# The narrow column block of two SwiGLU FFNs moved from last to first, and four seven-product units in every other wide block

## The chip, the cores and the metric

The kernel runs on one core of one Trainium2 chip. The metric is the device time in microseconds; lower is better. Engines are named as in the profile: PE (TensorE matmul), PEld (its weight load), DVE (VectorE), ACT (ScalarE), POOL (GpSimd) and SP (SyncE, which here only issues DMAs).

## The reference, cut to what matters

One layer on 256 tokens of width 2048: a SwiGLU half-step (FFN1), a token mixer, and a second SwiGLU half-step (FFN2). Everything is float32.

```python
D_MODEL, SEQ, D_FF = 2048, 256, 5504
def swiglu(x, w_gate, w_up, w_down):
    return (jax.nn.silu(x @ w_gate) * (x @ w_up)) @ w_down

f1 = swiglu(rms_norm(h, ffn1_pre_norm), ffn1_w_gate, ffn1_w_up, ffn1_w_down)
h = h + 0.5 * rms_norm(f1, ffn1_post_norm)
m = hybrid_token_mixer(rms_norm(h, mix_pre_norm), ...)      # not touched here
h = h + rms_norm(m, mix_post_norm)
f2 = swiglu(rms_norm(h, ffn2_pre_norm), ffn2_w_gate, ffn2_w_up, ffn2_w_down)
h = h + 0.5 * rms_norm(f2, ffn2_post_norm)
```

5504 is 10 x 512 + 384, so ten wide blocks of columns and one narrow one cover the gate and up matrices.

## The kernel before, in words

**Products.** A float32 product is made of three passes (`mm3`, L156 to L160): every operand is split into a rounded part `hi` (ACT, L152 and L279 to L285) and a rest `lo` (DVE, L154 and L244), and PE adds hi x hi, lo x hi and hi x lo. Tokens come in two tiles t of 128. The stationary operand is a 128x128 piece of the transposed input x (`xhi`, `xlo`), and the moving one a row of weights 512 (or 384) columns wide (`whi`, `wlo`). Weights come by DMA into `raw` (issued on SP), five buffers deep (`RING`), as do `whi` and `wlo`; so the splits can run five loads ahead of PE.

**One block of columns.** `gemm_pair` works on gate and up columns f0 to f0+w at once. The inner dimension is 16 pieces of 128, in eight units of two. A plain unit is 8 products, 24 matmuls. A unit with seven products (`Blocks.seven`) treats 2 token tiles x 2 inner pieces x 2 matrices (gate, up) as a two by two block product with seven products instead of eight: 21 matmuls, for which DVE and ACT form sums of weights (`wsum`, `wsumh`, `wsuml`) and the sums of x (`operand_sums`, kept as `hkhi`, `hklo`) must be there. `SUMS` are three such units (2, 4, 6) and `FOUR` are four (2, 4, 5, 6). `share` and `close` add the shared products into the accumulators `c` at a block's end.

**The order of blocks.** `ffn` goes through f0 = 0, 512, ..., 5120; the narrow block is the last. The first block of each FFN has plain units alone, since the sums of x are formed while it runs: 192 matmuls. In FFN1 (`begin` is given) it is a `gemm_pair` whose first loads are issued at the program's start by `begin`, while x is loaded, transposed and normalised piece by piece (`first_norm`). In FFN2 the gate half goes first through all inner pieces for t=0 and then for t=1 (`gemm_block` with `held`), while the norm of t=1 still runs, and the up half follows. After that, FFN1 has `SUMS` in blocks 1, 3, 5, 7, 9 and `FOUR` in 2, 4, 6, 8 and 10 (the narrow one); FFN2 has `FOUR` in 1, 3, 5, 7, 9 and `SUMS` in 2, 4, 6, 8 and 10 (narrow). A `SUMS` block is 183 matmuls, a `FOUR` block 180.

**After a block.** `finish` multiplies silu(gate) by up on DVE (L704), splits the result into 16 bit halves (ACT, L708), transposes them by a DMA that ACT issues (`turned`, L712), and copies them into `hT` (ACT, L717). `side` spreads such steps over the loads of the next block. Behind the last block there is no next block: `side.flush()` in `down_proj` takes the remaining steps after its second load. `down_proj` then multiplies `hT` by the down weights, inner piece by inner piece; pieces 6 and 7 are its first unit with seven products.

**What sets the order.** The program is written as above, and a scheduler gives each engine its queue, in order, when the kernel is built. A queue's instructions run in order, so one that waits holds up those behind it.

Of the kernel before, what the change touches and what calls it, by code (L numbers as in the profile page):

```python
# [7 lines left out]
F32 = mybir.dt.float32  # L8
# [8 lines left out]
P = 128  # L17
D = 2048
NT = 2
KT = D // P  # L20
DFF = 5504
FKT = DFF // P
EPS = 1e-6
CB = 512
GATE_NORMALIZER = 16.0
# [7 lines left out]
SUMS = (2, 4, 6)  # L33
FOUR = (2, 4, 5, 6)
# [53 lines left out]
def kernel(ctx: ExitStack, tc: tile.TileContext, a: dict, out: bass.AP):  # L88
# [15 lines left out]
    def nm(s):  # L104
        uid[0] += 1
        return f"{s}_{uid[0]}"
# [217 lines left out]
    def first_of(w_dram, c0, w=CB):  # L324
        def chunk(i):
            return wchunk(w_dram[2 * i * P:2 * (i + 1) * P, c0:c0 + w]
                          .rearrange("(k p) c -> p k c", p=P), w)
        return chunk
# [59 lines left out]
    def rstd(ss, n, width, tag):  # L388

        v = small.tile([P, width], F32, tag=f"{tag}v", name=nm("v"))  # L390
        nc.gpsimd.tensor_scalar(v, ss, 1.0 / n, EPS, op0=ALU.mult, op1=ALU.add)
        r = small.tile([P, width], F32, tag=f"{tag}r", name=nm("r"))
# [283 lines left out]
    def ffn(pre, x, rs, post, pre_next, begin=None, ready=(), then=None):  # L676
        with ExitStack() as fctx:
            fwork = fctx.enter_context(tc.tile_pool(name=nm("fwork"), bufs=2, reuse_waits="tile"))
            fpool = fctx.enter_context(tc.tile_pool(name=nm("fpool"), bufs=1, reuse_waits="tile"))
# [10 lines left out]
            raws = begin(x_sums) if begin else ()  # L690
# [4 lines left out]
                return [(hi, lo)]  # L695

            xl = lhs_of(x)
            hT = []

            fours = 0 if begin else 1  # L700

            def finish(t, f0, w, u, s):
                n = w // P
# [12 lines left out]
                src = turned[:, :2 * n, :].rearrange("p (h j) k -> p h j k", h=2)  # L716
                nc.scalar.activation(dst.rearrange("p j (k h) -> p h j k", h=2), src, AF.Copy)  # L717

            for f0 in range(0, DFF, CB):
                w = min(CB, DFF - f0)  # L720
                f1 = f0 + w
                w1 = min(CB, DFF - f1)
                following = [first_of(a[pre + s], f1, w1) for s in ("_w_gate", "_w_up") if w1]
                if f0 or begin:
                    g, u, ready = gemm_pair(
                        [(a[pre + "_w_gate"], f0), (a[pre + "_w_up"], f0)], w, xl, sums, ready,
                        following, () if f0 else raws,
                        (FOUR if f0 // CB % 2 == fours else SUMS) if f0 else ())
                else:
                    g = gemm_block(a[pre + "_w_gate"], f0, w, xl, held=held, ready=ready)  # L730
                    ready = ()
                s = []
                for t in range(NT):
                    st = fwork.tile([P, CB], F32, tag="silu", name=nm("silu"))
                    nc.scalar.activation(st[:, :w], g[t][:, :w], AF.Silu, scale=rs[t])
                    s.append(st)
                if not (f0 or begin):
                    side.spawn(x_sums())
                    u = gemm_block(a[pre + "_w_up"], f0, w, xl)
                hT.append(fpool.tile([P, 4, NT * P], F32, tag="hT", name=nm("hT"), bufs=11))  # L740
                for t in range(NT):
                    side.spawn(finish(t, f0, w, u[t], s[t]))
            def lhs():
                parts = {}

                def get(t, kt):
                    g2 = kt // 2
                    if g2 not in parts:
                        n = min(2, FKT - g2 * 2)
                        hi, lo = new_part(0), new_part(1)  # L750
# [34 lines left out]
            def ys():  # L785
                return fwork.tile([P, CB], F32, tag=ytags.pop(), name=nm("y"))

            return down_proj(a[pre + "_w_down"], FKT, lhs, sums_of, post, pre_next,
                             [wpost[:, n, :] for n in range(4)], ys,
# [488 lines left out]
    x, rs = new_xT(), [None, None]  # L1278

    def begin(x_sums):  # L1280

        raws = []

        def load_h(*tns):
            for t, n in tns:
                nc.sync.dma_start(h[t][n], a["x"][t * P:(t + 1) * P, n * CB:(n + 1) * CB])

        def load_w(*ics):
            for i, c in ics:
                raws.append(wload(a[("ffn1_w_gate", "ffn1_w_up")[i]]  # L1290
                                  [2 * c * P:2 * (c + 1) * P, :CB]
                                  .rearrange("(k p) c -> p k c", p=P), CB, apart=not (i or c)))

        load_h((0, 0))
        load_w((0, 0))
        load_h((1, 0))
        load_w((1, 0), (0, 1))
        load_h((0, 1))
        load_w((1, 1))
        load_h((1, 1))  # L1300
        load_w((0, 2))
        load_h((0, 2), (1, 2), (0, 3), (1, 3))

        idle = work.tile([P, CB], F32R, tag="tmp", name="idle", bufs=3)
        nc.gpsimd.memset(idle.bitcast(F32), 0.0)
        ps = ps_tile()

        def idling(n):
            for _ in range(n):
                nc.tensor.matmul(ps, lhsT=idle[:, :P], rhs=idle, start=True, stop=True)  # L1310

        idling(9)
        tp = ps_tile()
        nc.tensor.transpose(tp[:, :KT], wrow, ident[:KT, :KT])
        first_ops.append(nc.vector.tensor_copy(wcol, tp[:, :KT]))
        side.spawn(first_norm(x, rs, idling, x_sums))
        return raws

    x, rs, ready = ffn("ffn1", x, rs, "ffn1_post_norm", wcols[:, 1, :], begin,
                       then=first_of(a["w_in"], O_GQ))  # L1320
    x, rs, ready = mixer(x, rs, ready, first_of(a["ffn2_w_gate"], 0))
    ffn("ffn2", x, rs, "ffn2_post_norm", None, ready=ready)
    side.flush()

# [45 lines left out]
```

## Time and profile before

| | us |
|---|---|
| median of 3 runs | 2069.73 (2069.12 to 2075.82) |
| the profiled execution: time | 2072.41 |
| the profiled execution: span from the first to the last instruction | 2070.3 |
| PE busy | 2054.9 |
| DVE busy | 1849.8 |
| ACT busy | 1303.3 |

The times are device microseconds of whole executions; the span is that of the one profiled execution. A stretch "A:B" is in microseconds from the span's start. In a row of the timeline stand the start, the duration, the engine, the line, the operation, what it writes and reads, how many are merged, and in brackets how long the engine idled before it and what ended that. A matmul's duration is longer than the distance to the next one, since they overlap in the array; the distance of two starts is what one costs.

### The profile page before, as it was taken

The page shows a single profiled execution, that of the slowest core. Times are in us where ns is not written, and L with a number is a line of the kernel's source. Part 1 is how long each engine was busy: PE and PEld are TensorE (multiplying, and loading weights), DVE is VectorE, ACT ScalarE, POOL GpSimd, SP SyncE. Part 2 cuts the span into 40 slices and gives each one's busy share as a digit, 9 for nine tenths or more (in the row PEclk, how much of TensorE's full clock was granted, in tenths as well). Part 3 has the DMA queues.
Part 4 walks back from the last instruction along what each step waited for, and adds up shares of the span by engine and source line. Part 5 has one row for each costly group of instructions (what it writes and reads, how often), then busy time and mean ns, then how long its engine had stood idle before and what let it go on. Part 6 is the DMA issues. An engine that isn't in the chain of part 4 may idle for free. (4 is left out here: it accounts for less than half of the span.)

```text
span 2070.3 us, 28990 instructions
## 1 busy us (share of the span) xinstructions
PE 2054.9 (99%) x10337; PEld 1701.7 (82%) x10337; DVE 1849.8 (89%) x2187; ACT 1303.3 (63%) x1714; POOL 40.7 (2%) x87
## 2 busy tenths in 40 slices
PE   9999999999999999999999999999999999999998
PEld 7888888888888888878888888888888888888886
DVE  7899998998999879989999897577998999989996
ACT  6666666666666576576655554465666666666663
POOL 1000000000000100000000000010000000000000
PEclk9999999999999999999999999999999999999999
DMA  8776767767667467556565566756767767686663
GB/s 268 204 221 209 242 187 222 217 189 236 212 197 229 153 193 231 163 169 191 171 200 192 180 220 216 220 187 183 219 212 210 214 213 244 176 239 196 217 209 130
DMA packets 246105, 423.50 MB, mean 205 GB/s; under 512 B 63476, under 2 KB 71863, under 8 KB 245960
## 3 DMA queue, kind: packets, MB, share of 16 engines
q1 hardware_dynamic: 194896, 401.80, 61.6%
q10 hardware_dynamic: 51064, 19.84, 4.8%
q8 instruction: 81, 1.33, 0.3%
q14 instruction: 64, 0.52, 0.1%
HBM read 406.11 MB, written 4.19 MB: 198 GB/s over the span
## 5 line engine op out<-in xcount | busy, mean ns | idle before, releaser
L154 DVE TENSOR_TENSOR wlo<-raw,whi 128x1024 fp32r<-128x1024 f32 (+3 forms) x498 | 586.0, 1191 | 83.6 <-ACT whi L152 82.5
L152 ACT ACTIVATE whi<-raw 128x1024 fp32r<-128x1024 f32 (+3 forms) x498 | 507.1, 1031 | 228.9 <-PE c L159 66.2
L158 PE MATMUL c<-whi,xhi 128*128 128x512 f32 (+1 forms) x1270 | 494.0, 389 | 0.0
L160 PE MATMUL c<-wlo,xhi 128*128 128x512 f32 (+1 forms) x1270 | 490.7, 387 | 0.4 <-DVE wlo L154 0.4
L159 PE MATMUL c<-whi,xlo 128*128 128x512 f32 (+1 forms) x1270 | 490.4, 386 | 0.0
L244 DVE TENSOR_TENSOR wlo<-raw,whi 128x1024 fp32r<-128x1024 f32 (+1 forms) x252 | 295.9, 1204 | 35.9 <-ACT whi L283 23.1
L160 PEld LDWEIGHTS c<-wlo,xhi 128*128 128x128 f32 x1270 | 238.4, 188 | 48.0 <-DVE wlo L154 0.9
L158 PEld LDWEIGHTS c<-whi,xhi 128*128 128x128 f32 x1270 | 238.4, 188 | 46.6 <-ACT xhi L470 0.6
L159 PEld LDWEIGHTS c<-whi,xlo 128*128 128x128 f32 x1270 | 238.5, 188 | 45.6
L283 ACT ACTIVATE whi<-raw 128x1024 fp32r<-128x1024 f32 (+1 forms) x126 | 131.6, 1044 | 199.1 <-DVE raw L244 99.6
L244 DVE TENSOR_TENSOR wsuml<-wsum,wsumh 128x1536 fp32r<-128x1536 f32 (+1 forms) x126 | 217.9, 1729 | 8.1 <-ACT wsumh L285 8.1
L160 PE MATMUL c<-wlo,hkhi 128*128 128x512 f32 x558 | 217.2, 389 | 2.4 <-DVE wlo L154 2.0
L159 PE MATMUL c<-whi,hklo 128*128 128x512 f32 x558 | 216.9, 389 | 0.2 <-DVE hklo L154 0.2
L158 PE MATMUL c<-whi,hkhi 128*128 128x512 f32 x558 | 216.8, 389 | 0.0
L281 ACT ACTIVATE wsumh<-wsum 128x1024 fp32r<-128x1024 f32 (+1 forms) x126 | 131.1, 1040 | 88.3 <-DVE wsum L244 65.9
L279 ACT ACTIVATE whi<-raw 128x1024 fp32r<-128x1024 f32 (+1 forms) x126 | 130.9, 1039 | 60.0 <-PE c L159 44.9
L244 DVE TENSOR_TENSOR wsum<-raw,raw 128x1024 f32<-128x1024 f32 (+1 forms) x126 | 151.7, 1204 | 17.8 <-DMA raw<-in_ffn_w_down_dram 13.1
L160 PEld LDWEIGHTS c<-wlo,hkhi 128*128 128x128 f32 x558 | 104.7, 188 | 25.4 <-DVE wlo L154 2.4
L159 PEld LDWEIGHTS c<-whi,hklo 128*128 128x128 f32 x558 | 104.7, 188 | 22.2 <-DVE hklo L154 0.6
L158 PEld LDWEIGHTS c<-whi,hkhi 128*128 128x128 f32 x558 | 104.7, 188 | 21.4
L244 DVE TENSOR_TENSOR c<-c,psum 128x512 f32<-128x512 f32 (+1 forms) x135 | 86.4, 683 | 10.6 <-PE c L160 10.4
L244 DVE TENSOR_TENSOR wsum<-raw 128x512 f32<-128x512 f32 (+1 forms) x126 | 86.1, 683 | 3.6
(346 smaller groups left out, 3156.8 us busy)
## 6 DMA issues: line engine op xcount, KB each, us to landing
raw<-in_ffn_w_down_dram SPq DMA_DIRECT2D x124, 512.0 KB, 5.1
raw<-in_w_in_dram SPq DMA_DIRECT2D x104, 512.0 KB, 4.5
raw<-in_ffn_w_up_dram SPq DMA_DIRECT2D x97, 512.0 KB, 4.4
raw<-in_ffn_w_gate_dram SPq DMA_DIRECT2D x96, 512.0 KB, 4.7
raw<-in_ffn_w_gate_dram SPq DMA_DIRECT2D x128, 256.0 KB, 4.0
raw<-in_w_in_dram SPq DMA_DIRECT2D x128, 256.0 KB, 3.5
raw<-in_ffn_w_up_dram SPq DMA_DIRECT2D x126, 256.0 KB, 3.8
raw<-in_ffn_w_down_dram SPq DMA_DIRECT2D x96, 256.0 KB, 3.6
```

Source lines behind the costliest of these rows:

```text
L152: last[0] = nc.scalar.activation(hi, src, AF.Copy)
L154: nc.vector.tensor_tensor(lo, src, hi.bitcast(F32), op=ALU.subtract)
L158: nc.tensor.matmul(ps, lhsT=xhi, rhs=whi, start=start, stop=False)
L159: nc.tensor.matmul(ps, lhsT=xlo, rhs=whi, start=False, stop=False)
L160: nc.tensor.matmul(ps, lhsT=xhi, rhs=wlo, start=False, stop=stop)
L244: return nc.vector.tensor_tensor(o, x, y, op=op)
L279: nc.scalar.activation(ahi, ra, AF.Copy)
L281: nc.scalar.activation(hi[:, 0:2, :], wsum[:, 0:2, :], AF.Copy)
L283: nc.scalar.activation(bhi, rb, AF.Copy)
```

## The change

Both FFNs take the 384 wide block (columns 5120 to 5503) first and then the ten wide ones. Blocks are counted by j, their place in the order: block 0 is narrow and plain; blocks 1, 3, 5, 7, 9 have `FOUR`, blocks 2, 4, 6, 8, 10 `SUMS`, in both FFNs. The loads at the program's start and those that the mixer issues ahead for FFN2 are those of the narrow block.

```diff
+FIRST = DFF // 512 * 512
...
-            hT = []
-            fours = 0 if begin else 1
+            hT = {}
+            blocks = [FIRST] + list(range(0, FIRST, CB))
...
-            for f0 in range(0, DFF, CB):
+            for j, f0 in enumerate(blocks):
                 w = min(CB, DFF - f0)
-                f1 = f0 + w
-                w1 = min(CB, DFF - f1)
-                following = [first_of(a[pre + s], f1, w1) for s in ("_w_gate", "_w_up") if w1]
-                if f0 or begin:
+                following = [first_of(a[pre + s], f1) for f1 in blocks[j + 1:j + 2]
+                             for s in ("_w_gate", "_w_up")]
+                if j or begin:
                     g, u, ready = gemm_pair(
                         [(a[pre + "_w_gate"], f0), (a[pre + "_w_up"], f0)], w, xl, sums, ready,
-                        following, () if f0 else raws,
-                        (FOUR if f0 // CB % 2 == fours else SUMS) if f0 else ())
+                        following, () if j else raws, (FOUR if j % 2 else SUMS) if j else ())
...
-                hT.append(fpool.tile([P, 4, NT * P], F32, tag="hT", name=nm("hT"), bufs=11))
+                hT[f0 // CB] = fpool.tile([P, 4, NT * P], F32, tag="hT", name=nm("hT"), bufs=11)
...
-                                  [2 * c * P:2 * (c + 1) * P, :CB]
+                                  [2 * c * P:2 * (c + 1) * P, FIRST:]
...
-    x, rs, ready = mixer(x, rs, ready, first_of(a["ffn2_w_gate"], 0))
+    x, rs, ready = mixer(x, rs, ready, first_of(a["ffn2_w_gate"], FIRST, DFF - FIRST))
```

Line numbers of the changed kernel are mostly one higher (L154 becomes L155, L244 becomes L245). Of units with seven products FFN1 had 31 wide and 4 narrow ones, FFN2 32 wide and 3 narrow; each now has 35 wide ones. Every engine issues as many instructions as before; 21 matmuls that were 512 columns wide are now 384 wide.

Three places in the queues matter below. In the rows, `c`, `p` are accumulators in PSUM, `raw` loaded weights, and the numbers are the builder's.

DVE around the start of FFN1's second block, before: the sums of x (`sums`, `hklo`) are through ahead of the first block's product with silu (L704).

```order
L154 TENSOR_TENSOR hklo_569<-sums_501,hkhi_568 128x512
L207 TENSOR_TENSOR sums_630<-sums_572,sums_630 128x128
L154 TENSOR_TENSOR wlo_577<-raw_574,whi_576 128x1024
L154 TENSOR_TENSOR wlo_583<-raw_580,whi_582 128x1024
L154 TENSOR_TENSOR hklo_654<-sums_630,hkhi_653 128x512
L154 TENSOR_TENSOR wlo_638<-raw_635,whi_637 128x1024
L244 TENSOR_TENSOR wsum_681<-raw_679,raw_680 128x1024
L244 TENSOR_TENSOR raw_680<-wsum_681,raw_679 128x512
L154 TENSOR_TENSOR wlo_664<-raw_661,whi_663 128x1024
L704 SCALAR_TENSOR_TENSOR silu_586<-c_17_154,r_414,silu_586 128x512
```

And now, the same place on DVE:

```order
L155 TENSOR_TENSOR hklo_569<-sums_501,hkhi_568 128x512
L206 SCALAR_TENSOR_TENSOR sums_630<-sums_630,sums_572 128x128
L245 TENSOR_TENSOR wsum_663<-raw_661,raw_662 128x1024
L155 TENSOR_TENSOR wlo_583<-raw_580,whi_582 128x1024
L705 SCALAR_TENSOR_TENSOR silu_586<-c_17_154,r_414,silu_586 128x384
L705 SCALAR_TENSOR_TENSOR silu_588<-c_19_156,r_421,silu_588 128x384
L208 TENSOR_TENSOR sums_630<-sums_572,sums_630 128x128
L155 TENSOR_TENSOR wlo_638<-raw_635,whi_637 128x1024
L245 TENSOR_TENSOR raw_662<-wsum_663,raw_661 128x512
L245 TENSOR_TENSOR wsum_663<-raw_662 128x512
L245 TENSOR_TENSOR wlo_671<-raw_661,whi_670 128x1024
L155 TENSOR_TENSOR hklo_654<-sums_630,hkhi_653 128x512
```

The third load of the second block (`wlo_638`) and the last sums of x now stand behind the product with silu, which waits for the first block's last matmul.

DVE at the end of FFN1's gate and up work, before: one load of the down weights (`wlo_4115`) is split ahead of the closing of the block, the next three behind it.

```order
L154 TENSOR_TENSOR wlo_4115<-raw_4112,whi_4114 128x1024
L244 TENSOR_TENSOR psum_4064<-psum_4064,p_812_3842 128x384
L244 TENSOR_TENSOR c_789_3762<-c_789_3762,psum_4064 128x384
L244 TENSOR_TENSOR psum_4065<-psum_4064,p_811_3841 128x2x384
L244 TENSOR_TENSOR c_791_3764<-c_791_3764,psum_4064 128x384
L244 TENSOR_TENSOR c_790_3763<-c_790_3763,psum_4065 128x384
L244 TENSOR_TENSOR c_792_3765<-c_792_3765,psum_4065 128x384
L704 SCALAR_TENSOR_TENSOR silu_4098<-c_790_3763,r_414,silu_4098 128x384
L704 SCALAR_TENSOR_TENSOR silu_4100<-c_792_3765,r_421,silu_4100 128x384
L154 TENSOR_TENSOR wlo_4137<-raw_4134,whi_4136 128x1024
L154 TENSOR_TENSOR wlo_4165<-raw_4162,whi_4164 128x1024
L154 TENSOR_TENSOR wlo_4187<-raw_4184,whi_4186 128x1024
```

And now (`wlo_4115` is the row just before these):

```order
L155 TENSOR_TENSOR wlo_4137<-raw_4134,whi_4136 128x1024
L245 TENSOR_TENSOR psum_4064<-psum_4064,p_816_3866 128x512
L155 TENSOR_TENSOR wlo_4165<-raw_4162,whi_4164 128x1024
L245 TENSOR_TENSOR psum_4064<-psum_4064,p_818_3868 128x512
L155 TENSOR_TENSOR hklo_4278<-hT_1306,hkhi_4277 128x512
L245 TENSOR_TENSOR psum_4065<-psum_4064,p_817_3867 128x1024
L245 TENSOR_TENSOR c_792_3770<-c_792_3770,psum_4064 128x512
L245 TENSOR_TENSOR c_794_3772<-c_794_3772,psum_4064 128x512
L245 TENSOR_TENSOR c_793_3771<-c_793_3771,psum_4065 128x512
L155 TENSOR_TENSOR wlo_4187<-raw_4184,whi_4186 128x1024
L245 TENSOR_TENSOR c_795_3773<-c_795_3773,psum_4065 128x512
L705 SCALAR_TENSOR_TENSOR silu_4098<-c_793_3771,r_414,silu_4098 128x512
```

Four loads of the down weights are split ahead of the product with silu, where one was.

ACT at the same place, before (`whi_4259` and `wsumh_4253` belong to the first seven-product unit of the down weights):

```order
L708 ACTIVATE halves_4156<-silu_4100 128x768
L712 DMA_TRANSPOSE turned_4154<-halves_4152 128x6x128
L712 DMA_TRANSPOSE turned_4158<-halves_4156 128x6x128
L152 ACTIVATE whi_4234<-raw_4232 128x1024
L717 ACTIVATE hT_4102<-turned_4154 128x2x3x128
L717 ACTIVATE hT_4102<-turned_4158 128x2x3x128
L279 ACTIVATE whi_4259<-raw_4250 128x1024
```

And now:

```order
L709 ACTIVATE halves_4156<-silu_4100 128x1024
L713 DMA_TRANSPOSE turned_4154<-halves_4152 128x8x128
L713 DMA_TRANSPOSE turned_4158<-halves_4156 128x8x128
L153 ACTIVATE held_4207<-sums_4202 128x512
L153 ACTIVATE whi_4234<-raw_4232 128x1024
L718 ACTIVATE hT_4102<-turned_4154 128x2x4x128
L718 ACTIVATE hT_4102<-turned_4158 128x2x4x128
L280 ACTIVATE whi_4259<-raw_4250 128x1024
```

The order is the same but for `held_4207`; the transposes and the copies into `hT` are a third larger.

More of the change, by code (lines that the diff above doesn't have):

```diff
@@ L736, in ffn @@
                     s.append(st)
-                if not (f0 or begin):
+                if not (j or begin):
                     side.spawn(x_sums())
                     u = gemm_block(a[pre + "_w_up"], f0, w, xl)
-                hT.append(fpool.tile([P, 4, NT * P], F32, tag="hT", name=nm("hT"), bufs=11))
+                hT[f0 // CB] = fpool.tile([P, 4, NT * P], F32, tag="hT", name=nm("hT"), bufs=11)
                 for t in range(NT):
@@ L1290, in load_w @@
                 raws.append(wload(a[("ffn1_w_gate", "ffn1_w_up")[i]]
-                                  [2 * c * P:2 * (c + 1) * P, :CB]
-                                  .rearrange("(k p) c -> p k c", p=P), CB, apart=not (i or c)))
+                                  [2 * c * P:2 * (c + 1) * P, FIRST:]
+                                  .rearrange("(k p) c -> p k c", p=P), DFF - FIRST,
+                                  apart=not (i or c)))
         load_h((0, 0))
```

## The prediction

> **What bounds the kernel.** I read the page first, then the distance of matmul starts in the timeline, then the stretches of the single blocks, and last the waits at the blocks that move.
>
> ```profile
> span 2070.3 us, 28990 instructions
> PE 2054.9 (99%) x10337; PEld 1701.7 (82%) x10337; DVE 1849.8 (89%) x2187; ACT 1303.3 (63%) x1714; POOL 40.7 (2%) x87
> PEclk9999999999999999999999999999999999999999
> ```
>
> PE is busy nearly throughout at a clock that is always granted, so time is saved by fewer or shorter matmuls, or by taking out places where PE waits. DVE, at 89%, is the next engine. What one matmul costs is the distance of starts in an undisturbed piece. The first and the last of 72 wide ones, and of 24 narrow ones:
>
> ```profile
> 1712.25 0.39 PE L158 MATMUL c<-whi,xhi 128*128 128x512 f32 x1
> 1728.34 0.39 PE L160 MATMUL c<-wlo,xhi 128*128 128x512 f32 x1
> 454.31 0.33 PE L158 MATMUL c<-whi,xhi 128*128 128x384 f32 x1
> 458.29 0.33 PE L160 MATMUL c<-wlo,xhi 128*128 128x384 f32 x1
> ```
>
> A wide one costs 16.09/71 = 0.2266 us, a narrow one 3.98/23 = 0.1730; 128 columns are worth 0.054. With these prices every block can be checked. The stretches run from a block's first matmul to the next one's; FFN1's rows come first (block 0, 1, 9, the narrow block, the first six pieces of the down product, its first seven-product unit), then FFN2's (block 0, 1, 2, 3, narrow, the six pieces, the unit).
>
> ```profile
> core 0: us, PE busy (x) PEld busy (x) DVE busy (x) ACT busy (x) POOL busy (x), PEclk, DMA share, GB/s
> 7.11:54.32 47.21, 47.21 (x221) 38.71 (x221) 41.73 (x59) 34.73 (x56) 6.22 (x10) 1.00 0.83 277
> 54.32:96.25 41.93, 41.93 (x187) 34.47 (x185) 34.56 (x36) 26.08 (x29) 0.00 (x0) 1.00 0.78 217
> 383.89:425.37 41.48, 41.48 (x185) 34.35 (x183) 39.73 (x43) 27.25 (x32) 0.00 (x0) 1.00 0.74 216
> 425.37:458.47 33.10, 32.31 (x182) 31.09 (x180) 30.82 (x41) 23.86 (x32) 0.00 (x0) 1.00 0.65 183
> 458.47:477.13 18.66, 16.65 (x73) 13.44 (x73) 13.43 (x21) 12.49 (x16) 0.00 (x0) 1.00 0.67 204
> 477.13:482.36 5.23, 5.15 (x22) 3.79 (x21) 5.23 (x5) 3.04 (x4) 0.00 (x0) 1.00 0.77 246
> 1383.09:1429.06 45.97, 45.97 (x213) 37.92 (x212) 40.23 (x53) 29.47 (x45) 5.66 (x12) 1.00 0.57 172
> 1429.06:1470.65 41.59, 41.39 (x181) 33.63 (x180) 33.75 (x33) 25.32 (x27) 0.00 (x0) 1.00 0.68 198
> 1470.65:1512.13 41.48, 41.48 (x184) 34.36 (x183) 39.47 (x41) 28.19 (x32) 0.00 (x0) 1.00 0.76 233
> 1512.13:1552.93 40.80, 40.80 (x181) 33.79 (x180) 38.67 (x40) 27.33 (x31) 0.00 (x0) 1.00 0.66 200
> 1800.17:1832.92 32.75, 32.34 (x184) 31.59 (x183) 30.20 (x39) 23.81 (x33) 0.00 (x0) 1.00 0.75 214
> 1832.92:1849.49 16.57, 16.53 (x74) 13.34 (x73) 11.78 (x20) 8.84 (x12) 0.00 (x0) 1.00 0.96 222
> 1849.49:1856.03 6.54, 5.76 (x22) 3.81 (x22) 5.87 (x6) 6.54 (x9) 0.00 (x0) 1.00 0.76 258
> ```
>
> A wide `SUMS` block is 183 x 0.2266 = 41.47 us and takes 41.48; a wide `FOUR` block is 180 x 0.2266 = 40.79 and takes 40.80. Both lose nothing, though DVE is at 95% to 96% in them. The narrow block of FFN1 is 180 x 0.1730 = 31.14 and takes 33.10: 1.96 lost. That of FFN2 is 183 x 0.1730 = 31.66 and takes 32.75: 1.09 lost. Then 72 matmuls of the down product (16.32) take 18.66 in FFN1 and 16.57 in FFN2, and 21 (4.76) take 5.23 and 6.54; lost there are 2.34 + 0.47 = 2.8 and 0.25 + 1.78 = 2.0. FFN2's block 1 loses 41.59 - 40.79 = 0.8. All that this change can reach is about 11 us.
>
> **The change, part by part.**
>
> *Columns.* Seven units with seven products go from narrow to wide, so 21 matmuls more are spared in wide blocks and 21 fewer in narrow ones: 21 x 0.054 = 1.1 us less on PE, which is the path. Both ends are 1.1. The Trainium skill (TensorE: Matmul & The Clock Gate, Back-to-back issue gap) gives sustained spacings of about 81 ns for 128 columns and 131 ns for 512 in streams with weight loads; an estimate along that line makes 128 columns 17 ns and this term 0.35 us. The trace, at 227 and 173 ns, disagrees.
>
> *The narrow block without shared products.* Its losses of 1.96 and 1.09 stood at its units with seven products, which it no longer has:
>
> ```profile
> L160 PE MATMUL p<-wsuml,hkhi 128*128 128x384 f32 x8 | 3.0, 376 | 0.8 <-DVE wsuml L244 0.8
> ```
>
> The weights' sums came late from DVE. In their place stand one more wide `SUMS` block in each FFN and, in FFN1, `FOUR` in other blocks, which in the rows above lose 0.0. I take -3.1; the weak end is -2.7 (0.2 left in each).
>
> *The end of gate and up.* Now a wide `SUMS` block ends both FFNs. The copies into `hT` have no next block to hide in; on ACT they wait for the transposing DMA, with the first seven-product unit's split (L279) queued behind them, and DVE and PE wait for that. FFN1's 2.0 us was another wait, for the second load of the down weights, whose rest stood behind the product with silu on DVE. The rows: FFN1's wait; FFN2's chain; two wide blocks' chains.
>
> ```profile
> 464.08 0.50 PE L160 MATMUL c<-wlo,hkhi 128*128 128x512 f32 x1 [2.01 <-DVE wlo L154]
> 1837.22 2.58 ACTq L712 DMA_TRANSPOSE turned<-halves  x2
> 1845.58 1.07 ACT L717 ACTIVATE hT<-turned 128x768 uint16<-128x768 uint16 x1 [4.09 <-DMA turned<-halves]
> 1847.46 1.07 ACT L717 ACTIVATE hT<-turned 128x768 uint16<-128x768 uint16 x1 [0.81 <-DMA turned<-halves]
> 1848.40 1.03 ACT L279 ACTIVATE whi<-raw 128x1024 fp32r<-128x1024 f32 x1
> 1555.61 2.99 ACTq L712 DMA_TRANSPOSE turned<-halves  x2
> 1566.10 1.37 ACT L717 ACTIVATE hT<-turned 128x1024 uint16<-128x1024 uint16 x1 [2.14 <-DMA turned<-halves]
> 1679.95 2.66 ACTq L712 DMA_TRANSPOSE turned<-halves  x2
> 1686.11 2.57 ACT L717 ACTIVATE hT<-turned 128x1024 uint16<-128x1024 uint16 x2
> ```
>
> In FFN1 the order moves three loads of down weights ahead of silu, so the 2.0 us should go; FFN1 is then as FFN2 is. FFN2's chain from issue to the last copy was 1848.54 - 1837.22 = 11.3 us and cost 2.0. Wide chains took 8.7 (1688.68 - 1679.95) to 11.9 (1567.47 - 1555.61): nothing lost at the fast end, 2.0 + 0.6 at the slow one. I take 1.5 in each FFN, inside these, so 4.8 becomes 3.0: -1.8. The ends are 0 in each (-4.8) and 4 in each (+3.2, if the wide block's larger closing work on DVE delays the issue too).
>
> *The start of FFN1.* Block 0 becomes 192 x 0.054 = 10.4 us shorter on PE. DVE's 16 splits there fall only by a quarter, while the norm's pieces and the sums of x stay; and `FOUR` follows at once, one unit with seven products more than before. The DVE rows of a split, wide and narrow, and of the parts of such a unit:
>
> ```profile
> L154 DVE TENSOR_TENSOR wlo<-raw,whi 128x1024 fp32r<-128x1024 f32 x462 | 557.1, 1219 | 72.6 <-ACT whi L152 71.7
> L154 DVE TENSOR_TENSOR wlo<-raw,whi 128x768 fp32r<-128x768 f32 x18 | 16.7, 950 | 2.4 <-ACT whi L152 2.4
> L244 DVE TENSOR_TENSOR wsuml<-wsum,wsumh 128x1536 fp32r<-128x1536 f32 x119 | 208.4, 1751 | 7.9 <-ACT wsumh L285 7.9
> L244 DVE TENSOR_TENSOR wsum<-raw,raw 128x1024 f32<-128x1024 f32 x119 | 145.0, 1219 | 16.3 <-DMA raw<-in_ffn_w_down_dram 13.1 <-DMA raw<-in_w_in_dram 1.5 <-PE c L160 1.2
> L244 DVE TENSOR_TENSOR wsum<-raw 128x512 f32<-128x512 f32 x119 | 82.2, 691 | 3.4
> L244 DVE TENSOR_TENSOR raw<-wsum,raw 128x512 f32<-128x512 f32 x119 | 82.0, 689 | 2.5
> ```
>
> The narrow splits save 16 x 0.27 = 4.3 us; the extra unit costs 1.22 + 0.69 + 0.69 + 2 x 1.22 + 1.75 - 2 x 1.22 = 4.35. DVE keeps 41.73 + 34.56 = 76.3 us in blocks 0 and 1, and PE has 36.8 + 41.1 = 77.9 instead of 89.1: 98%. At the 95.8% (39.73 of 41.48) that costs PE nothing, DVE needs 79.6, 1.7 more than there is. Five loads of lead can hide that, so the low end is 0. If block 0 also keeps its DVE waits (47.21 - 41.73 = 5.5, on transposes and norms), DVE needs 83.4: 5.5 lost. I take 1.2, nearer to FFN2's block 1, a `FOUR` block behind plain units, at 0.8.
>
> *The start of FFN2.* DVE goes from 74.0 us in 87.6 to 69.7 in 76.4, 91%; the 0.8 stays. The pass over t=0, under which the norm of t=1 runs, is 48 x 0.054 = 2.6 us shorter: I take 0.4 for that, between 0 and 2; with the 0.8 itself gone the low end is -0.8.
>
> *Loads.* As many DMAs as before, in the same order on SP; their DMA share is 0.57 to 0.83 in the blocks concerned, and narrow loads bring less for a shorter block. Nothing, while the share stays under 1.
>
> The sum: -1.1 - 3.1 - 1.8 + 1.2 + 0.4 = -4.4 us. Of the profiled execution (span 2070.3, time 2072.4, 2.1 around it) that leaves 2068.0. It stood 2.7 over the median of the three runs, 2069.7; taken from the median, 2065.3. All low ends together make -9.8 (2059.9), all high ends +7.3 (2077.0).
>
> **The rivals.**
>
> *The end costs nothing.* With DVE ahead by four loads and transposes as in the fast row, both ends lose 0: -1.1 - 3.1 - 4.8 + 1.2 + 0.4 = -7.4, 2062.3. For it: the fast chain is 2.6 us shorter than FFN2's, more than the 2.0 lost. Against it: the DMA share behind FFN2's block was 0.96, and it may be as full again.
>
> *The end costs as much or more.* Slow transposes and bigger closing work in both FFNs, 3.7 each: -1.1 - 3.1 + 2.6 + 1.6 = 0.0, 2069.7. For it: larger transposes. Against it: three of four rows of the chain lie under it.
>
> *DVE's debt at the starts: slower than before.* If FFN1's start loses 5.5 and FFN2's 2.0, the sum is -1.1 - 3.1 - 1.8 + 7.5 = +1.5, 2071.2. It decides once both starts together lose over 6.0. For it: 98% of DVE, and the last sums of x now behind silu in DVE's queue. Against it: FFN2 does much the same at its start for 0.8.
>
> **How the numbers follow.** A measurement of this kernel tells about 0.3%, 6.2 us, from no change. The forecast, 2063.5 to 2068, has 0.47; the free end 0.24, nearly all of it faster by over 0.3%; the costly end 0.17 and DVE's debt 0.12, both mostly within 0.3%. Faster 0.25, same 0.68, slower 0.07 (debt and costly end together). Eight in ten lie from 2061.5 to 2072.0.
>
> **What would show it.** Narrow blocks at the starts, about 36.8 and 36.0 us long; ten blocks behind each at 40.8 and 41.5; the first `FOUR` block up to 1 over 40.8, with PE waits on `wsuml`; no PE wait of 2 us behind FFN1's last block; ACT still waiting for `turned` ahead of the first down unit. I am wrong if a `FOUR` or `SUMS` block behind the second loses over 0.5, if block 0 takes over 39, or if the down product's first 93 matmuls lose over 4 in either FFN.

## The result, and the profile after

The changed kernel took 2065.25 us (median of 7 runs, 2063.12 to 2067.47) beside 2073.58 for the kernel before (7 runs, 2069.12 to 2076.20). The ratio is 0.9968, with a 95% interval from 0.9959 to 0.9978: about 6.6 us faster, between 4.6 and 8.5 (the two medians by themselves are 8.3 apart). The profiled execution took 2066.25 us, with a span of 2064.3, which is 6.0 under that of before. Forecast were 2065.3 us and 4.4 us under the profiled execution.

```profile
span 2064.3 us, 28994 instructions
PE 2051.2 (99%) x10337; PEld 1702.9 (82%) x10337; DVE 1858.0 (90%) x2187; ACT 1304.9 (63%) x1714; POOL 41.1 (2%) x87
```

PE still bounds the kernel and DVE is still next. The stretches of the changed kernel, cut as in the prediction: FFN1's block 0 (narrow), 1 (`FOUR`), 9 (`FOUR`) and 10 (`SUMS`), the first six pieces of its down product and its first seven-product unit; then FFN2's block 0 and 1, the six pieces and the unit.

```profile
7.38:44.10 36.72, 36.72 (x222) 36.21 (x221) 33.46 (x53) 28.70 (x53) 7.29 (x10) 1.00 0.84 273
44.10:85.39 41.29, 41.29 (x184) 33.90 (x184) 39.68 (x42) 27.64 (x33) 0.00 (x0) 1.00 0.72 220
373.70:415.12 41.42, 41.42 (x181) 33.62 (x180) 39.32 (x40) 28.03 (x31) 0.00 (x0) 1.00 0.65 190
415.12:456.61 41.49, 41.49 (x185) 34.35 (x184) 40.04 (x43) 28.11 (x33) 0.00 (x0) 1.00 0.77 231
456.61:472.92 16.31, 16.31 (x73) 13.51 (x72) 12.05 (x18) 11.70 (x14) 0.00 (x0) 1.00 0.75 197
472.92:477.68 4.76, 4.76 (x22) 3.94 (x21) 4.76 (x5) 4.76 (x7) 0.00 (x0) 1.00 0.89 243
1379.19:1415.88 36.69, 36.37 (x213) 35.33 (x212) 33.69 (x51) 26.50 (x44) 4.92 (x12) 1.00 0.58 172
1415.88:1458.94 43.06, 41.73 (x182) 33.56 (x181) 36.77 (x36) 24.38 (x27) 0.00 (x0) 1.00 0.72 205
1830.08:1846.39 16.31, 16.31 (x73) 13.51 (x72) 12.72 (x19) 12.37 (x15) 0.00 (x0) 1.00 0.66 164
1846.39:1851.15 4.76, 4.76 (x22) 3.94 (x21) 4.76 (x5) 3.71 (x5) 0.00 (x0) 1.00 0.93 321
```

"Lost" is, here and below, a stretch less its matmuls at 0.2266 and 0.1730 us. Both ends (16.31 and 4.76) lose nothing at all, though a wide block closes ahead of them. The new loss stands in FFN2's block 1: 43.06 where 180 matmuls take 40.8. Block 9 loses 0.6 in both FFNs. The whole span, in us:

| stretch | before | after | difference |
|---|---|---|---|
| up to FFN1's first matmul | 7.11 | 7.38 | +0.27 |
| FFN1's eleven blocks | 451.36 | 449.23 | -2.13 |
| FFN1's down product, first 93 matmuls | 23.89 | 21.07 | -2.82 |
| the rest of it, and the mixer | 900.73 | 901.51 | +0.78 |
| FFN2's eleven blocks | 449.83 | 450.89 | +1.06 |
| FFN2's down product, first 93 matmuls | 23.11 | 21.07 | -2.04 |
| the rest | 214.27 | 213.15 | -1.12 |

In the last row what PE lost at the down product's fourth seven-product unit (1.1 us before) is gone too. In FFN1, whose row holds the mixer as well, the later units of the down product lost 2.7 instead of 1.15; but the run below with FFN1 changed in the same way lost only 0.2 there. That row lay between 898.7 and 901.8 in the thirteen traces of this study. So a difference of two spans carries up to 3 us of chance, and the experiments are read by stretches, each in one profiled execution.

### The profile page after: what moved, and what is told of

It reads as the page before. It is cut to its first block, busy times and chain, and to the rows that moved or that the text cites. A ratio compares the mean times of both kernels' runs of the same rounds, so it can differ in the third digit from the quotient of the medians.

```text
span 2064.3 us, 28994 instructions
## 1 busy us (share of the span) xinstructions
PE 2051.2 (99%) x10337; PEld 1702.9 (82%) x10337; DVE 1858.0 (90%) x2187; ACT 1304.9 (63%) x1714; POOL 41.1 (2%) x87
## 5 line engine op out<-in xcount | busy, mean ns | idle before, releaser
L155 DVE TENSOR_TENSOR wlo<-raw,whi 128x1024 fp32r<-128x1024 f32 (+3 forms) x498 | 582.8, 1184 | 70.9 <-ACT whi L153 70.0
L245 DVE TENSOR_TENSOR wlo<-raw,whi 128x1024 fp32r<-128x1024 f32 x252 | 299.4, 1218 | 36.9 <-ACT whi L284 23.6
L284 ACT ACTIVATE whi<-raw 128x1024 fp32r<-128x1024 f32 x126 | 133.1, 1057 | 201.2 <-DVE raw L245 95.0
L245 DVE TENSOR_TENSOR wsuml<-wsum,wsumh 128x1536 fp32r<-128x1536 f32 x126 | 220.6, 1751 | 8.0 <-ACT wsumh L286 8.0
L282 ACT ACTIVATE wsumh<-wsum 128x1024 fp32r<-128x1024 f32 x126 | 132.6, 1053 | 92.7 <-DVE wsum L245 70.7
L280 ACT ACTIVATE whi<-raw 128x1024 fp32r<-128x1024 f32 x126 | 132.4, 1051 | 60.8 <-PE c L160 49.4
L245 DVE TENSOR_TENSOR wsum<-raw,raw 128x1024 f32<-128x1024 f32 x126 | 153.4, 1218 | 18.2 <-DMA raw<-in_ffn_w_down_dram 15.7
L245 DVE TENSOR_TENSOR c<-c,psum 128x512 f32<-128x512 f32 x135 | 87.4, 690 | 11.5 <-PE c L161 11.2
L245 DVE TENSOR_TENSOR wsum<-raw 128x512 f32<-128x512 f32 x126 | 87.0, 690 | 3.6
```

The lines of the kernel that those rows point to most:

```text
L155: nc.vector.tensor_tensor(lo, src, hi.bitcast(F32), op=ALU.subtract)
L245: return nc.vector.tensor_tensor(o, x, y, op=op)
L280: nc.scalar.activation(ahi, ra, AF.Copy)
L282: nc.scalar.activation(hi[:, 0:2, :], wsum[:, 0:2, :], AF.Copy)
L284: nc.scalar.activation(bhi, rb, AF.Copy)
```

## Experiments

Every ratio is to runs of the kernel before on the same chip. Two readings had to be told apart at each place: that a short block or a heavy `FOUR` block gives DVE too little time, or that a few instructions stand at a bad place in an engine's queue.

### The start of FFN2: the copies of block 0

In the changed kernel's timeline ACT waits for the transposed tile of block 0, with the split (L280) of block 1's next seven-product unit queued behind; DVE waits for that split, and PE, later, for the weights' sums.

```profile
1418.48 2.77 ACTq L713 DMA_TRANSPOSE turned<-halves  x2
1426.55 1.08 ACT L718 ACTIVATE hT<-turned 128x768 uint16<-128x768 uint16 x1 [4.20 <-DMA turned<-halves]
1427.50 1.03 ACT L280 ACTIVATE whi<-raw 128x1024 fp32r<-128x1024 f32 x1
1428.56 1.23 DVE L245 TENSOR_TENSOR wlo<-raw,whi 128x1024 fp32r<-128x1024 f32 x1 [3.62 <-ACT whi L280]
1435.62 0.50 PE L161 MATMUL p<-wsuml,hkhi 128*128 128x512 f32 x1 [0.72 <-DVE wsuml L245]
1443.99 0.50 PE L161 MATMUL p<-wsuml,hkhi 128*128 128x512 f32 x1 [0.60 <-DVE wsuml L245]
```

The edit is one ordering edge in the changed kernel (`last[0]` is then the last split of the second unit's sums, `FIRST` the narrow block's column):

```diff
-                nc.scalar.activation(dst.rearrange(...), src, AF.Copy)
+                with tc.issue_after(last[0].ins) if f0 == FIRST else nullcontext():
+                    nc.scalar.activation(dst.rearrange(...), src, AF.Copy)
```

> The changed kernel, with the two copies of block 0 into hT put behind the sums of the next seven-product unit in ACT's queue (one edge that orders them; ACT alone changes, 8 rows in FFN2). Theory A (FFN2's loss in block 1 comes from ACT, which waits 4.2 us for the transposed tile with the split L280 queued behind it, so that DVE waits 3.6 us for that split): ACT's wait goes or falls under 1 us, DVE's 3.6 us wait too, and block 1 falls from 43.06 to 41.3 or less; about 1.8 us under the changed kernel, ratio to before about 0.996. Theory B (DVE simply has more work than the short blocks give time for): block 1 keeps 42.5 to 43, and the wait on wsuml only changes its place.

Measured: ratio 0.9964 (0.9952 to 0.9977). Two rows of ACT and the stretch of block 1:

```profile
1421.64 1.04 ACT L280 ACTIVATE whi<-raw 128x1024 fp32r<-128x1024 f32 x1
...
1429.48 1.98 ACT L719 ACTIVATE hT<-turned 128x768 uint16<-128x768 uint16 x2
```

```profile
1415.06:1455.90 40.84, 40.84 (x181) 33.80 (x181) 37.95 (x38) 25.59 (x30) 0.00 (x0) 1.00 0.76 225
```

Counted from the block's start the split runs 5.0 us earlier, the copies wait for nothing, and block 1 takes 40.84: 2.2 of the 2.26 was this wait. In the two later runs that keep this edit block 1 loses 0.05 too. A `FOUR` block behind the short block 0 is not too much for DVE.

### One FFN alone

FFN1 as changed, FFN2 as before.

```diff
-            blocks = [FIRST] + list(range(0, FIRST, CB))
+            blocks = [FIRST] + list(range(0, FIRST, CB)) if begin else list(range(0, DFF, CB))
```

> FFN1 as in the changed kernel, FFN2 as before. If the parts add up as the two traces stand (FFN1 and its down product and what follows up to FFN2: -3.9 us; FFN2's blocks: +1.1; its down product: -3.2), this is 3.9 us under before, ratio 0.998, with FFN2's blocks at 45.97, 41.6 and a narrow last one at 32.8, and 2 us lost behind it. If the second FFN's gain depends on what the first one leaves (loads, queue positions), its rows differ from those of before by over 0.5 us.

Measured: ratio 0.9979 (0.9967 to 0.9990), some 4.4 us (2.1 to 6.8). FFN2's narrow block took 32.67, the six pieces 16.94, the unit 6.54, so its end lost 0.62 + 1.78 = 2.4 as before; its block 1 took 40.8 instead of 41.6, so the 0.8 of the kernel before isn't there in every execution. Within this noise the gains of the two FFNs add up.

### The end: what kind of block stands last

Four kernels change which blocks have which units, and the last of them also where the narrow block stands. The two kinds exchanged, so that a wide `FOUR` block is last:

```diff
-                        ..., (FOUR if j % 2 else SUMS) if j else ())
+                        ..., (SUMS if j % 2 else FOUR) if j else ())
```

> The narrow block first as in the change, but SUMS in wide blocks 1, 3, 5, 7, 9 and FOUR in 2, 4, 6, 8, 10 of both FFNs: the same matmuls, the heavier units one block later, and a FOUR block last. Theory A (the free ends come from the narrow block with seven-product units being gone, and the loss behind FFN2's block 0 from ACT waiting for the transposed tile with a split queued behind it): the first 93 matmuls of both down products lose under 0.5 us as in the change; FFN2's block 1, now 183 matmuls (41.47), still loses 0.7 to 1.2 at its first seven-product unit, against 2.26. Time about 1 us under the changed kernel, ratio to before 0.996 to 0.9965. Theory B (FOUR is too much for DVE wherever DVE has no lead): FFN2's block 1 loses nothing (41.5), but DVE has no lead at the end, and each end loses 2 to 3 us again: about 3 us over the changed kernel, ratio 0.998.

Measured: ratio 0.9974 (0.9963 to 0.9986). FFN2's block 1 took 41.52, no loss, against theory A: its first seven-product unit comes one plain step later, which may be cover enough. The ends lost 2.9 and 4.0, against theory A too. The stretches of the two first units (4.76 without a loss), and DVE in the second:

```profile
473.22:479.99 6.77, 5.54 (x23) 3.79 (x21) 6.71 (x8) 5.62 (x7) 0.00 (x0) 1.00 0.71 207
1845.08:1853.78 8.70, 6.98 (x23) 5.16 (x22) 8.64 (x10) 6.80 (x9) 0.00 (x0) 0.80 0.73 235
```

```profile
1842.69 1.23 DVE L245 TENSOR_TENSOR wsum<-raw,raw 128x1024 f32<-128x1024 f32 x1 [4.49 <-DMA raw<-in_ffn_w_down_dram]
```

DVE waits for the unit's own weights: their loads were issued 4 to 7 us after the down product began, where the changed kernel issues them 5 to 3 us ahead of it. A buffer for a load comes free when DVE has split what it held: SyncE waited 7.6 us in FFN1 and 6.8 in FFN2 for a split on DVE (L155), which stood behind the last block's product with silu (L705). So a DVE that is behind makes its loads late too. The last block, `FOUR`, also holds three splits of the down product's operand, which matter below; a run with `FOUR` last and these splits later was not made.

The kernel before with a plain narrow block as the last:

```diff
-                        (FOUR if f0 // CB % 2 == fours else SUMS) if f0 else ())
+                        (FOUR if f0 // CB % 2 == fours else SUMS) if f0 and w == CB else ())
```

> The kernel before, with plain units in the narrow block, which stays last: 12 narrow matmuls more in FFN1 and 9 in FFN2, 21 x 0.173 = 3.6 us more on PE. Theory A (the losses in the narrow block and behind it are one debt, which its seven-product units run up on DVE): the 3.05 us lost in the two blocks go, and the down products' first 93 matmuls lose under 1 us in each FFN against 2.8 and 2.0: 3.6 - 3.05 - 4 = about 3.5 us under before, ratio 0.998 to 0.9985. Theory B (the down product waits since a short block ends the FFN, whose closing steps have less time to hide in): the ends lose 4.8 as before; 0.5 us over before, ratio 1.000.

Measured: ratio 0.9980 (0.9971 to 0.9989), as theory A had it. Narrow block and six pieces of FFN1:

```profile
425.65:458.96 33.31, 33.31 (x194) 33.30 (x192) 19.05 (x24) 20.07 (x23) 0.00 (x0) 1.00 0.76 223
458.96:475.32 16.36, 16.36 (x74) 13.52 (x73) 11.66 (x13) 12.00 (x14) 0.00 (x0) 1.00 0.82 205
```

With DVE at 19 us in 33, a narrow last block loses 0.1 (33.31 less 192 x 0.1730; 0.5 in FFN2), and the end 0.04. So a short block at the end is no harm in itself. The scheduler changed one more thing here: of the splits of the down product's operand (`hklo`), of which the kernel before has three in FFN1's narrow block and two in FFN2's, this one has none and one.

The last two blocks of the first of these four kernels in the other order, so that `SUMS` is last:

```diff
-                        ..., (SUMS if j % 2 else FOUR) if j else ())
+                        ..., (FOUR if j in (2, 4, 6, 8, 9) else SUMS) if j else ())
```

> As the run with the two kinds of block exchanged (SUMS first), but with the last two wide blocks in the other order: FOUR in 2, 4, 6, 8, 9 and SUMS in 1, 3, 5, 7, 10 of both FFNs. The counts of matmuls are those of the changed kernel. Theory A (the units of the last block alone decide what the end costs: behind SUMS the loads of the first seven-product unit of the down product are issued 3 to 5 us before that product starts, behind FOUR 4 to 7 us after it): the first 93 matmuls of both down products lose under 0.3 us, against 2.9 and 4.1; the two FOUR blocks in a row lose 0.3 to 1.5. With FFN2's block 1 at 41.5 that makes about 2 us less than the changed kernel, ratio to before about 0.996. Theory B (the lead is a sum over the whole FFN, and SUMS at the start or two FOUR in a row use it up): the ends still lose over 1.5 each; time as the changed kernel or above.

Measured: ratio 0.9993 (0.9982 to 1.0004), a miss: neither the gain of theory A nor two costly ends. The loads were ahead (by 3.0 to 0.9 us, and 3.9 to 1.8), and FFN1's end lost nothing. The second `FOUR` in a row lost 1.0 and 0.7. But FFN2's first unit took 7.31 and lost 2.55:

```profile
1843.96 1.37 ACT L718 ACTIVATE hT<-turned 128x1024 uint16<-128x1024 uint16 x1 [4.30 <-DMA turned<-halves]
1847.20 1.23 DVE L245 TENSOR_TENSOR wlo<-raw,whi 128x1024 fp32r<-128x1024 f32 x1 [7.34 <-ACT whi L284]
```

The second transposed tile landed 15.7 us after the down product began (10.5 in the changed kernel), and the unit's other splits stood behind its copy. So early loads are not enough. Why the tile landed that late is open.

The narrow block in the middle (the sixth of eleven), with `FOUR`; a wide `SUMS` block last:

```diff
-            for f0 in range(0, DFF, CB):
+            wide = list(range(0, DFF - DFF % CB, CB))
+            blocks = wide[:5] + [wide[-1] + CB] + wide[5:]
+            for j, f0 in enumerate(blocks):
...
-                        (FOUR if f0 // CB % 2 == fours else SUMS) if f0 else ())
+                        (FOUR if j % 2 else SUMS) if f0 else ())
```

> The kernel before with the narrow block as the sixth of eleven (j = 5) in both FFNs, block 0 wide and plain, FOUR in odd places (the narrow block too) and SUMS in even ones, a wide SUMS block last. FFN1 has the matmuls of before, FFN2 three narrow ones fewer and three wide ones more. Theory A (a narrow block with four seven-product units needs about 31 us of DVE in 31.1 of PE, so it loses wherever it stands): it takes 33 us, 1.5 to 2 lost, in each FFN, and since a wide SUMS block is last both ends are free: about 3 us under before, ratio 0.9985. Theory B (its losses belong to the end of the FFN; in the middle the lead from a SUMS block hides it): under 0.6 lost in it; about 6 us under before, ratio 0.997.

Measured: ratio 0.9974 (0.9965 to 0.9983). The narrow blocks of FFN1 and FFN2:

```profile
218.89:250.38 31.49, 31.49 (x181) 31.20 (x180) 29.39 (x37) 22.10 (x28) 0.00 (x0) 1.00 0.71 209
1588.59:1620.00 31.41, 31.41 (x182) 31.18 (x180) 29.36 (x36) 22.80 (x29) 0.00 (x0) 1.00 0.72 212
```

They lose 0.35 and 0.27, where the same block lost 1.96 as FFN1's last. Both ends are free, but for 0.2 in FFN2. DVE has 37 instructions here and had 41 there, 29.39 us against 30.82. Theory B: the loss belongs to the end of the FFN. What FFN1's narrow block has lost from DVE's queue by moving are three instructions of the down product. In the kernel before:

```profile
440.05 0.68 DVE L154 TENSOR_TENSOR hklo<-hT,hkhi 128x512 fp32r<-128x512 f32 x1
...
446.58 0.68 DVE L154 TENSOR_TENSOR hklo<-hT,hkhi 128x512 fp32r<-128x512 f32 x1
...
450.11 0.68 DVE L154 TENSOR_TENSOR hklo<-hT,hkhi 128x512 fp32r<-128x512 f32 x1
```

### The queue at the end: ACT's copies

The two copies of the last block put behind the sums of the down product's first unit (`summed[0]` is the last split of these sums), in the kernel before and in the one with `FOUR` last:

```diff
-                nc.scalar.activation(dst.rearrange(...), src, AF.Copy)
+                with tc.issue_after(summed[0].ins) if f0 + w == DFF else nullcontext():
+                    nc.scalar.activation(dst.rearrange(...), src, AF.Copy)
...
-                if not hf and kt == 1:
+                if not hf and kt == 1:
+                    side.pump()
+                    side.pump()
+                if not hf and kt == 8:
                     side.flush()
```

> The kernel before; behind the last block the two copies into hT are put behind the sums of the down product's first seven-product unit in ACT's queue (their data is needed only at inner piece 38 and later). Theory A (the 2.0 us lost in FFN2 come from ACT, which waits 4.9 us for the transposed tiles with that unit's splits queued behind it): the down product's first unit in FFN2 loses under 0.4 instead of 1.78, and less of the 1.16 behind it is lost too; FFN1 keeps its 2.2 us wait for the second load, which is another wait: 2 to 3 us under before, ratio 0.9985 to 0.999. Theory B (the unit's loads, issued 2.4 us after the down product begins, are what comes late): 1.5 or more stays lost there.

Measured: ratio 0.9980 (0.9971 to 0.9989). FFN1's six pieces, FFN2's six pieces and unit:

```profile
458.64:477.55 18.91, 16.66 (x74) 13.45 (x74) 14.02 (x22) 11.09 (x15) 0.00 (x0) 1.00 0.65 201
...
1831.04:1847.40 16.36, 16.36 (x73) 13.52 (x73) 15.90 (x23) 13.31 (x17) 0.00 (x0) 1.00 0.94 252
1847.40:1852.16 4.76, 4.76 (x22) 3.94 (x21) 4.76 (x8) 2.84 (x5) 0.00 (x0) 1.00 0.93 339
```

FFN2's 2.0 is gone with the loads as late as before, so it was ACT's order. FFN1 keeps its 2.6: another wait, as theory A had it.

> The run with SUMS first and FOUR last, with the same edit of ACT's order behind the last block. There the loads of the down product's first unit were issued 4.3 to 6 us after that product began and landed 13 to 14 after it. Theory A (the copies on ACT hold the splits): the 2.9 and 4.1 us lost at the ends fall under 0.7 each, and about 5 us are gained over that run, ratio to before 0.995. Theory B (FOUR last leaves DVE no lead, so the loads come late whatever ACT does): at least 1.5 stays lost in each, with DVE's wait for raw of 4 us still there; about 1.5 us gained.

Measured: ratio 0.9985 (0.9974 to 0.9995). The first units took 9.22 and 8.16; the ends lost 5.4 and 3.7, beside 2.9 and 4.0 without the edit (about 1.4 of the 5.4, and of the 4.0, is a slower clock; see the last section). Theory B holds for the cause, and its 1.5 us of gain did not come. With loads as late as these, ACT's order doesn't help.

### The queue at the end: DVE's splits

The kernel before, narrow block last and all units as they were; only the first three splits of the down product's operand are queued behind the weights' sums formed last (`weighed[0]`), which for its first half are the last block's:

```diff
-                        split_into(hi[:, :n, :], lo[:, :n, :], hT[g2 // 2][:, c:c + n, :])
+                        with tc.issue_after(weighed[0].ins) if g2 < 3 else nullcontext():
+                            split_into(hi[:, :n, :], lo[:, :n, :], hT[g2 // 2][:, c:c + n, :])
```

> The kernel before, with the splits of the down product's first operands (hklo from hT, three of 0.68 us on DVE, which the scheduler had put between the last block's work) queued behind the last block's last weights' sums. Theory A (the narrow block loses 1.96 and 1.09 as the last one because these splits are put into a block that has DVE at 95% already; in the middle it lost 0.35 and 0.27): the narrow blocks lose under 0.6 each, 2 us gained there; what the down product loses at its start stays (2.8 and 2.0) or grows by up to 1, since the splits now come later: 1 to 2 us under before, ratio 0.999 to 0.9995. Theory B (the narrow last block loses for another reason, the loads of the down weights or the closing work of the block ahead): it still loses over 1.5 and 0.9.

Measured: ratio 0.9975 (0.9964 to 0.9985). Narrow block, six pieces and unit of FFN1, then of FFN2:

```profile
425.51:456.93 31.42, 31.42 (x182) 31.18 (x181) 29.37 (x37) 24.00 (x32) 0.00 (x0) 1.00 0.69 207
456.93:473.29 16.36, 16.36 (x74) 13.51 (x73) 14.37 (x23) 11.76 (x17) 0.00 (x0) 1.00 0.68 204
473.29:478.43 5.14, 5.14 (x23) 3.79 (x21) 5.14 (x5) 2.94 (x4) 0.00 (x0) 1.00 0.86 234
1794.44:1826.83 32.39, 32.05 (x184) 31.71 (x183) 29.64 (x37) 23.67 (x32) 0.00 (x0) 1.00 0.76 220
1826.83:1843.19 16.36, 16.36 (x73) 13.51 (x73) 14.55 (x24) 12.48 (x17) 0.00 (x0) 1.00 0.71 215
1843.19:1847.95 4.76, 4.76 (x22) 3.94 (x21) 4.76 (x5) 2.37 (x4) 0.00 (x0) 1.00 0.92 300
```

The narrow block loses 0.3 instead of 1.96 in FFN1 and 0.7 instead of 1.1 in FFN2. And what was expected to stay goes as well: the down products lose 0.4 and 0.04 instead of 2.8 and 2.0. These stretches add up to 6.4 us, and the ratio gives 5.2 (3.1 to 7.5), with the narrow block still last. The three splits of FFN1 now stand at the block's closing and behind it:

```profile
453.77 0.69 DVE L155 TENSOR_TENSOR hklo<-hT,hkhi 128x512 fp32r<-128x512 f32 x1
...
461.13 0.68 DVE L155 TENSOR_TENSOR hklo<-hT,hkhi 128x512 fp32r<-128x512 f32 x1
...
464.81 0.69 DVE L155 TENSOR_TENSOR hklo<-hT,hkhi 128x512 fp32r<-128x512 f32 x1
```

Up to the closing DVE's queue in the block differs by these splits alone (on ACT a few splits changed places too), so what the narrow block gains is put down to them. They do no harm everywhere: the changed kernel has three of them in FFN1's last block, a wide `SUMS` one, which takes 41.49 and loses nothing.

```profile
L155 DVE TENSOR_TENSOR hklo<-hT,hkhi 128x512 fp32r<-128x512 f32 x3 | 2.1, 686 | 0.0
```

So it takes both, the splits and a block in which they leave DVE no room. What the down products gain is less clear. The edge is on DVE alone, but the scheduler moved more with it: a second load of the down weights is split ahead of FFN1's product with silu, where one was, and on ACT the first split of the unit stands ahead of the copies (in FFN2 at 1834.84, the first copy at 1835.79). FFN2's second transposed tile landed 10.8 us after the down product began, and 14.5 us after it in the kernel before. Which of these freed the ends was not separated.

### A version that is faster than both

The changed kernel with block 0's copies late, and a sixth `FOUR` block:

```diff
-                        ..., (FOUR if j % 2 else SUMS) if j else ())
+                        ..., (FOUR if j in (1, 3, 4, 6, 7, 9) else SUMS) if j else ())
```

> The changed kernel with block 0's copies put later, and a sixth FOUR block in each FFN: FOUR in 1, 3, 4, 6, 7, 9, SUMS in 2, 5, 8, 10. Three wide matmuls fewer in each FFN: 2 x 0.68 = 1.36 us less on PE. Theory A (DVE, at 95% over a FOUR and a SUMS block, has room for one more unit in three blocks, about 97%): two FOUR blocks in a row lose under 0.3, the ends stay free, 1 us under the run with the later copies, ratio to before about 0.996. Theory B (a FOUR block leaves no lead, so that a second one waits for its weights' sums): the second of each pair loses over 0.7, which with two pairs in each FFN is 2.8 or more: 1.4 us or more over the run with the later copies.

Measured: ratio 0.9954 (0.9942 to 0.9966). The second `FOUR` of a pair lost 0.14 and 0.36 in FFN1, 0.0 and 0.43 in FFN2: a little over theory A's 0.3 and under theory B's 0.7. Block 9 lost 0.5 and 0.3 there, 0.63 and 0.55 in the changed kernel, and 0.9 and 0.1 in the run with the copies late alone. All of these have one of those splits in it, between the parts of a unit; in the changed kernel at 404.38:

```profile
403.25 1.22 DVE L245 TENSOR_TENSOR wlo<-raw,whi 128x1024 fp32r<-128x1024 f32 x1
404.38 0.69 DVE L155 TENSOR_TENSOR hklo<-hT,hkhi 128x512 fp32r<-128x512 f32 x1
404.99 1.22 DVE L245 TENSOR_TENSOR wlo<-raw,whi 128x1024 fp32r<-128x1024 f32 x1
406.12 1.75 DVE L245 TENSOR_TENSOR wsuml<-wsum,wsumh 128x1536 fp32r<-128x1536 f32 x1
```

The last run adds to it the edit of DVE's splits.

> The run with six FOUR blocks in each FFN, with the same edit. Theory A (block 9 loses 0.3 to 0.5 there, and 0.6 in the changed kernel, because one split of the down product's operand, 0.69 us on DVE, stands between the parts of a seven-product unit): block 9 loses under 0.15 in both FFNs, the ends stay free; 0.5 us under that run, ratio to before about 0.995. Theory B (a FOUR block so near the end loses because of the loads): block 9 keeps its loss. If the splits come too late for the down product, its first pieces lose 0.5 or more, and the run is no faster.

Measured: ratio 0.9946 (0.9933 to 0.9960), median 2061.16. Block 9 of FFN1 and FFN2:

```profile
373.12:413.92 40.80, 40.80 (x182) 33.80 (x180) 38.70 (x40) 27.76 (x31) 0.00 (x0) 1.00 0.67 198
...
1742.58:1783.38 40.80, 40.80 (x181) 33.80 (x180) 38.29 (x39) 27.68 (x31) 0.00 (x0) 1.00 0.70 195
```

They lose nothing, the ends stay free, as theory A had it. Over the runs a wide `FOUR` block 9 behind a `SUMS` block lost 0.0 to 0.9 with such a split in it, and 0.01 where it had none (both FFNs here, and FFN2 of the run with DVE's splits put later). But FFN2's block 7 lost 1.1 in this execution, which was not followed up; the losses of blocks 1 to 10 of both FFNs add up to as much as without the edit. So block 9 is free, and that the kernel as a whole is faster than the one without the edit is not shown (0.9946 and 0.9954, with overlapping intervals). It has the lowest ratio of the kernels tried; its interval just touches that of the changed kernel.

## Why the prediction was right, and where only its sum was

The direction and the size are inside what was forecast, and so is the place of most of the time. Term by term, in us:

| term | forecast | measured |
|---|---|---|
| columns | -1.1 | -1.1 |
| the narrow block's losses | -3.1 | -3.05, and +0.8 come back in other blocks, most of all 9 |
| the end of gate and up | -1.8 | -4.8 |
| FFN1's start | +1.2 | -0.15 |
| FFN2's start | +0.4 | +2.5 |
| sum | -4.4 | -5.9 |

The rounded terms add up to -5.8; the rows of the table of stretches give -5.9.

*Columns.* Wide blocks stand at 41.48 and 40.80 as before, plain multiples of 0.2266, so the counts decide. Right.

*The narrow block.* The size was right and the reason was wrong, so the size is luck in part. The prediction read the wait on `wsuml` as a property of a narrow block with seven-product units. The narrow block in the middle (0.35) and the run with DVE's splits put later (0.3) show that it was these units together with the down product's splits in its queue. The splits moved along with the end of the FFN. One of them now falls into block 9, which loses 0.63 and 0.55 (in FFN2 blocks 5 and 9 of the kernel before lost 0.2 each): the 0.8 that the forecast did not have. The prediction had said that it would be wrong if a block behind the second lost over 0.5; by that sign its account of these blocks was.

*The end.* The mis-sized term. It was priced by the length of the transposes' chain, 11.3 us, with the two wide rows as its ends, and 1.5 was taken for each FFN; measured is 0 in both, the low end and the first rival. The chains took 8.4 us in FFN1 and 7.7 in FFN2, less than either of the two rows. And the chain is one of two conditions. With loads 4 to 7 us late it doesn't help when the copies run (5.4 and 3.7 lost); with early loads late copies alone cost 2.55. The changed kernel has both in time: its loads are issued 5 to 3 us ahead. Loads that were only up to 2.8 us late did no harm in FFN2 of the kernel before once the copies stood behind the splits. That the 2.0 us wait in FFN1 was a different one from FFN2's was right: the edit of ACT's order took away the one and left the other.

*FFN1's start.* DVE's 98% was taken for a near bound. DVE was busy for 73.1 of the 78.0 us of blocks 0 and 1, 94%, where the prediction had 76.3 of 77.9. Block 0 took 36.72 as forecast (36.8), block 1 lost 0.5 as before.

*FFN2's start.* This is the step that failed. It was given 0.4 for the norm's cover, while the mechanism that the prediction itself describes for the end, ACT waiting for `turned` with a split queued behind, was not looked for behind block 0. There it cost 2.2 of the 2.26 lost in block 1, where up to 1 was expected; block 0 was 1.0 longer than 45.97 less its columns. The rival of DVE's debt named this place and a price of 2.0, but not the cause: one ordering edge removes the loss.

The errors of the end (-3.0) and of the two starts (+2.1 and -1.35) and block 9 (+0.8) largely cancel, which is why the forecast of -4.4 stands near -5.9. That the time itself was met to 0.1 us is luck: the first three runs of the kernel before had a median 3.9 under that of all seven, from which the same -4.4 gives 2069.2, outside the band of the forecast. By the prediction's own line of 0.3%, 6.2 us, the 6.6 just count as faster, to which it gave 0.25.

Two sums of the prediction don't come out, and no term hangs on them: with its own 2 for FFN2's start all high ends make +6.9 and not +7.3, and the losses in its rows add up to 8.7 us, with the columns to 9.8, and not to about 11.

## What to carry to other kernels

Where an engine is at 95% and another waits for it, look in its queue for instructions that aren't due yet: three of 0.68 us, which a scheduler had placed early, cost 1.7 us in one block, and the order without them there gained 5 in the whole. Look also at what else the scheduler moves with an edit. Before a block is blamed for a loss, put it somewhere else: the same block lost 1.96 at the end and 0.35 in the middle. And when a mechanism is named at one place (a copy that waits for a DMA, with a split queued behind it), go through the program for every other place where the same instructions follow each other.

## What the hardware showed that was not expected

After two waits close to each other PE ran at half its rate for a while. In the kernel with `FOUR` last, in FFN2:

```profile
1845.98 0.50 PE L160 MATMUL p<-whi,hklo 128*128 128x512 f32 x1 [0.48 <-DVE hklo L155]
1847.72 0.75 PE L161 MATMUL p<-wlo,hkhi 128*128 128x512 f32 x1 [1.24 <-DVE wlo L245]
1848.26 0.63 PE L159 MATMUL c<-whi,held 128*128 128x512 f32 x1
1848.69 0.63 PE L160 MATMUL c<-whi,held 128*128 128x512 f32 x1
...
1851.24 0.40 PE L160 MATMUL p<-whi,held 128*128 128x512 f32 x1
1851.47 0.40 PE L161 MATMUL p<-wlo,held 128*128 128x512 f32 x1
```

```profile
1848.00:1852.00 4.00, 4.00 (x12) 3.13 (x12) 3.94 (x4) 3.24 (x5) 0.00 (x0) 0.60 0.88 237
```

From 1848.3 to 1851.2 starts are 0.427 us apart instead of 0.2266, at a granted clock of 0.60 over these 4 us (0.50 from 1847.80 to 1851.21); that is 1.4 us of the 3.94 lost there. The run with ACT's order changed as well showed it in FFN1 behind a wait of 2.44 us (0.52 granted), but not in FFN2 behind a wait of the same length; nor did FFN1's wait of 2.01 us in the kernel before bring it. The Trainium skill (TensorE: Matmul & The Clock Gate, What's actually happening) describes a gate that halves the clock after an idle window of about 3.4 us, with windows that run freely. The half rate and its length of about 3.4 us agree, and so does the chance in it; but here PE was idle for no more than 2.44 us at a stretch, so shorter waits can be enough. What sets it off was not tested. As an estimate, from the rows above, a wait of 2 us may cost 1.4 more.
